# Giving the rotated keys' and queries' tile 128 more bytes per partition, and with it other start addresses to what lies behind it

## The chip, the cores and the metric

The kernel runs on one NeuronCore of a Trainium2 chip. The metric is the device time of one execution in microseconds (us). TensorE (PE in the profile) multiplies matrices; VectorE (DVE), ScalarE (ACT) and GpSimd (POOL) work on elements; SyncE (SP) issues the transfers between the chip's memory (DRAM) and the on-chip buffer (SBUF, 128 partitions). An address in this document is a byte offset within a partition, and it is the same on all 128.

## The reference

The program is a two-layer decoder trunk for 256 tokens of width 1024, all in float32. Each layer is a half-step SwiGLU feed-forward (FFN), a token mixer, a second FFN and a gated input embedding, each followed by a scaled residual and a layer norm:

```python
for i in range(DEPTH):                       # DEPTH = 2
    if i == N_A:
        k_nope, k_rope, v_shared = shared_kv(x, ...)
    x = post_norm(x, 0.5 * swiglu(x, ffn1_w_in[i], ffn1_w_out[i]), ...)
    mix = fox_mixer(x, ...) if i < N_A else mla_mixer(x, ..., k_nope, k_rope, v_shared, cos, sin)
    x = post_norm(x, mix, ...)
    x = post_norm(x, 0.5 * swiglu(x, ffn2_w_in[i], ffn2_w_out[i]), ...)
    gate = sigmoid(x @ ple_w_gate[i] + ple_b_gate[i])
    x = post_norm(x, gate * (p[i] @ ple_w_proj[i]), ...)
```

Layer 0 mixes with forgetting attention (FoX: 16 heads of 64, a decay mask), layer 1 with multi-head latent attention (MLA: 16 heads, keys and values from a shared latent, 128 unrotated and 64 rotated dimensions). The FFN's inner width is 2816.

## The kernel before

**Numbers in two parts.** Every matrix is held as a high part, rounded to TensorE's float32r, and a low part, the rest. A product is three matmuls (`mm3`): high by high, high by low, low by high. Each weight unit arrives in one of three landing buffers (`raw`, 8,192 bytes per partition), ACT writes its high part (line 252) and DVE its low part (line 253) into a buffer of 8,448 bytes, and TensorE reads it from there, as the operand that it loads first (the stationary one) or as the one that streams past (the moving one). In the profile's names, `h<-xT,hl` has the moving operand first and the stationary one behind it. Nearly all matmuls are recorded at line 616, in the helper `mm`.

**The buffers.** Ten buffers (`hl0` to `hl9`) hold split weights only. Four more, named in `HOMES = ("fs", "qk", "ota", "otb")`, and `gb` change their use from stage to stage: now a split weight, now something else. In the FFNs (`ffn`, line 721, with `sums` at line 859) the inner width is cut into 11 chunks. For most chunks eight block sums of the activations (a scheme that needs seven products in place of eight) are put as high and low part in one of the four homes, and `sums` multiplies a chunk's sums, stationary, by the weights' sums, moving: seven products of three matmuls of 512 columns for each chunk, and the chunks take the homes in turn. The cold first FFN has five such chunks, of which one lies in `ota`; each of the three other FFNs has eight, in two groups of four, `fs`, `qk`, `ota`, `otb`. In both mixers `ota` and `otb` hold the attention's output (`OT`), stationary in the output product `O`: 96 matmuls of 512 columns in FoX, and 168 in MLA (its last two heads' outputs lie in `fs`).

**How addresses come about.** A pool gives each name (tag) one place, as large as the largest tile ever asked for under that name, rounded up to 32 bytes, and lays the names out in the order in which they are first asked for. So a tile's size sets where all later names begin. The largest tile under `qk` is the one in `gen` of the MLA stage: the rotated (and unrotated) keys and queries, `[128, 2, 1072]` of 4 bytes, 8,576 bytes, of which columns 0 to 1023 of each half are used. The other large buffers take 8,448 bytes, which is 33 times 256. Small unused tiles (`gap0` to `gap3`) and a shift by 48 words in `Stream.place` (for weights that are the moving operand beside `xT` in the FoX values and the first embedding gate) set other starts.

Start addresses before, modulo 256: `xT` 160; `fs`, `hl0` to `hl9`, `P`, `g4`, `gb`, `ts`, `qk` 224; `ota` (178,272) and `otb` (186,720) 96; `PT` (the transposed attention weights) 160; `p1` (a third block of them) 128; the three `raw` buffers 128.

The order of the work is that of the program text and of the tables `FOX` and `ORDER`; a planner in `Stream` decides, from costs in columns, after which matmul a weight unit is split.

Of the kernel before, what the change touches and what calls it, by code (L numbers as in the profile page):

```python
# [11 lines left out]
F32R = mybir.dt.float32r  # L12
# [498 lines left out]
class Trunk:  # L511
# [990 lines left out]
    def mla(self, li):  # L1502
# [173 lines left out]

        def gen(h):
            if h == 0:
                o = self.own([128, 2, 1072], F32R, "qk")
                home["qk"] = o[:, :, 0:1024].rearrange("p w (t i s c) -> p w t i s c", t=2, i=2, s=2)  # L1680
            ps = self.bank("h")
            hp, s = h // 2, h % 2
            w = self.use(("kvk", hp))
            for k in range(2):
                self.mm3(
                    ps[:, 256:512], lambda i: w[:, i, 256 * k + 128 * s : 256 * k + 128 * s + 128],
                    lambda i: self.ckv[:, :, i, k, :], k == 0, k == 1,
                )
            w = self.use(("qn", hp))
            for k in range(3):  # L1690
                self.mm3(
                    ps[:, 0:256], lambda i: w[:, i, 256 * k + 128 * s : 256 * k + 128 * s + 128],
                    lambda i: cqt[:, :, i, k, :], k == 0, k == 2,
                )
            o = home["qk"]
            left["gen", h] = o[:, :, :, 0, s], o[:, :, :, 1, s], ps.rearrange("p (w t c) -> p w t c", w=2, t=2)
# [108 lines left out]
        def hold(x):  # L1805
            S.hold = bool(x)

        steps = dict(
            dq=dq, rms=rms, dqs=dq_scale, cqT=cq_transpose, V=V, vlo=vlo, qr=q_rope, rope=rope, rc=rope_copy, rot=rotate, zT=zT_first,
            zs=z_split, zU=zT_last, gen=gen, QK=QK, mi=minima, ex=exps, rec=recip, div=divide, T=T, AV=AV,  # L1810
            ga=high("gen"), gd=low("gen"), ta=high("T"), tr=raw_copy, td=low("T"), oa=high("AV"), od=low("AV"), O=O, y=room, hold=hold,
            f=S.fill, a=S.ahead, l=S.later, XT=lambda t, n: self.XT(t, (n,)),
# [122 lines left out]
```

## Time and profile before

| | us |
|---|---|
| median of 3 runs | 1050.32 (1049.77 to 1051.04) |
| the profiled execution | 1049.6 |
| its span, first to last instruction | 1047.8 |
| TensorE busy with matmuls | 1035.6 |
| VectorE busy | 891.8 |
| ScalarE busy | 592.9 |

The granted TensorE clock is full (0.998 in the mean). A row of the profile's timeline gives the start of a group of instructions, its length, engine, line, operation, operands, shapes and count. Matmuls are pipelined: a matmul's own length runs beyond the start of the next one, so what a group costs is read from its start to the start of the group behind it.

### The profile page before, as it was taken

The numbers are of one execution on the slowest core, as the hardware profiler recorded it, in microseconds if no ns is written. First come the engines' busy times: TensorE is split into PE (matmuls) and PEld (weight loads), VectorE is DVE, ScalarE is ACT, GpSimd is POOL, SyncE is SP. The second block draws the span as 40 slices with busy tenths as digits, with TensorE's granted clock in tenths as the row PEclk, the third lists the DMA queues.
The fourth block names the chain that finished last, engine by engine and source line by source line (L and its number), as shares of the span: only waits on it lengthen the run. The fifth ranks groups of instructions, "written<-read, shape, count | busy, mean of one in ns | idle before, by whom it ended". The sixth has DMA issues, their size and how long they took to land.

```text
span 1047.8 us, 17555 instructions
## 1 busy us (share of the span) xinstructions
PE 1035.6 (99%) x7085; PEld 948.6 (91%) x7085; DVE 891.8 (85%) x1312; ACT 592.9 (57%) x901; POOL 58.0 (6%) x88
## 2 busy tenths in 40 slices
PE   9999999999999999999999999999999999999996
PEld 8999898899889999998899898988999889898986
DVE  5788977868898979978979899888887989889877
ACT  6555563666755555663565646646776564646541
POOL 0000000122300000000220000000000000000000
PEclk9999999999999999999999999999999999999999
DMA  7855586455636363673674545743445564555732
GB/s 281 305 191 188 185 298 243 162 168 169 216 128 246 121 252 125 241 282 132 236 260 151 195 169 190 270 142 112 145 156 179 183 214 162 200 190 176 271 125 81
DMA packets 37476, 202.74 MB, mean 193 GB/s; under 512 B 3970, under 2 KB 9874, under 8 KB 16532
## 3 DMA queue, kind: packets, MB, share of 16 engines
q1 hardware_dynamic: 37396, 201.63, 54.3%
q8 instruction: 55, 0.90, 0.3%
q14 instruction: 25, 0.20, 0.1%
HBM read 200.55 MB, written 1.06 MB: 192 GB/s over the span
## 4 chain that ended last, share of the span: by engine, by line
PE 95%; DVE 2%; ACT 1%; issue 1%; DMA 0%; SPq 0%; DVEq 0%; ACTq 0%
PE h L616 53%; PE y L616 29%; PE tr L616 10%; PE tr L620 2%; DVE hl L253 1%; PE h L620 1%; DMA raw<-in_w_dram 0%; PE tr L1375 0%; DVE ts L300 0%; DVE x L705 0%; DVE tr L1720 0%; ACT qk L629 0%; DVE PT L633 0%; DVE ts L306 0%; DVE raw L308 0%
## 5 line engine op out<-in xcount | busy, mean ns | idle before, releaser
L616 PE MATMUL h<-xT,hl 128*128 128x256 f32 x3144 | 366.1, 277 | 1.2 <-ACT hl L327 0.7
L616 PEld LDWEIGHTS h<-xT,hl 128*128 128x128 f32 x3144 | 362.0, 188 | 2.9 <-ACT hl L327 1.2
L253 DVE TENSOR_TENSOR hl<-raw,hl 128x1024 fp32r<-128x1024 f32 (+5 forms) x271 | 314.2, 1190 | 36.1 <-ACT hl L252 35.0
L252 ACT ACTIVATE hl<-raw 128x1024 fp32r<-128x1024 f32 (+5 forms) x271 | 267.8, 1027 | 70.6 <-DVE raw L308 41.3
L616 PE MATMUL y<-hl,g 128*128 128x512 f32 x336 | 78.6, 391 | 0.0
L616 PEld LDWEIGHTS y<-hl,g 128*128 128x128 f32 x336 | 62.5, 188 | 12.6
L616 PE MATMUL h<-hl,xT 128*128 128x512 f32 (+2 forms) x312 | 67.9, 371 | 0.0
L616 PEld LDWEIGHTS h<-hl,xT 128*128 128x128 f32 x312 | 54.9, 188 | 9.8
L616 PE MATMUL y<-hl,otb 128*128 128x512 f32 x219 | 58.0, 399 | 0.0
L264 DVE TENSOR_TENSOR hl<-raw,hl 128x1024 fp32r<-128x1024 f32 (+2 forms) x44 | 52.3, 1192 | 0.8 <-ACT hl L260 0.7
L616 PE MATMUL y<-hl,xT 128*128 128x512 f32 (+3 forms) x282 | 52.7, 334 | 0.0
L260 ACT ACTIVATE hl<-raw 128x1024 fp32r<-128x1024 f32 (+2 forms) x44 | 45.2, 1029 | 9.7 <-DVE raw L308 9.1
L629 ACT ACTIVATE xT<-tr 128x512 fp32r<-128x512 f32 x28 | 16.1, 597 | 58.9 <-PE tr L620 58.9
L616 PEld LDWEIGHTS y<-hl,xT 128*128 128x128 f32 x282 | 44.1, 188 | 4.6 <-ACT xT L629 0.4
L616 PEld LDWEIGHTS y<-hl,otb 128*128 128x128 f32 x219 | 39.8, 188 | 8.4 <-DVE otb L633 0.3
L616 PE MATMUL y<-hl,ota 128*128 128x512 f32 x177 | 46.8, 398 | 0.1
L700 POOL TENSOR_TENSOR rs<-ve,mhalf 128x1 f32<-128x1 f32 x16 | 15.1, 942 | 519.8 <-DVE ve L699 519.8
L616 PE MATMUL tr<-xT,hl 128*128 128x256 f32 x360 | 42.5, 277 | 0.0
L616 PEld LDWEIGHTS tr<-xT,hl 128*128 128x128 f32 x360 | 41.7, 188 | 0.4
L616 PEld LDWEIGHTS y<-hl,ota 128*128 128x128 f32 x177 | 32.7, 189 | 7.7 <-DVE hl L253 0.6
L823 ACT ACTIVATE P<-h 128x512 f32<-128x512 f32 x33 | 19.7, 596 | 33.0 <-PE h L616 32.6
L300 DVE TENSOR_TENSOR ts<-raw 128x1024 f32<-128x1024 f32 x29 | 35.4, 1222 | 0.6
(322 smaller groups left out, 1632.7 us busy)
## 6 DMA issues: line engine op xcount, KB each, us to landing
raw<-in_ffn_in_dram SPq DMA_DIRECT2D x85, 1024.0 KB, 5.0
raw<-in_ffn_out_dram SPq DMA_DIRECT2D x44, 1024.0 KB, 5.0
raw<-in_pg_dram SPq DMA_DIRECT2D x8, 1024.0 KB, 4.9
raw<-in_mo_dram SPq DMA_DIRECT2D x8, 1024.0 KB, 4.8
raw<-in_kq_dram SPq DMA_DIRECT2D x8, 640.0 KB, 4.2
gb<-in_ln_g_dram SPq DMA_DIRECT2D x8, 512.0 KB, 5.9
gb<-in_ln_b_dram SPq DMA_DIRECT2D x8, 512.0 KB, 7.5
raw<-in_fk_dram SPq DMA_DIRECT2D x4, 1024.0 KB, 5.6
```

Source lines behind the costliest of these rows:

```text
L252: nc.scalar.activation(hi, src, AF.Copy)
L253: nc.vector.tensor_tensor(lo, src, hi.bitcast(F32), op=ALU.subtract)
L260: nc.scalar.activation(hi, src, AF.Copy)
L264: nc.vector.tensor_tensor(lo, src, hi.bitcast(F32), op=ALU.subtract)
L300: tt(s[:, 0:1024].rearrange("p (a b) -> p a b", b=512), r[:, 0:512][:, None, :].to_broadcast([128, 2, 512]), r[:, 512:1536].rearrange("p ( ...
L616: self.nc.tensor.matmul(out, lhsT, rhs, start=start, stop=stop)
L620: self.nc.tensor.transpose(out, in_, self.ident)
L629: self.nc.scalar.activation(hi, src, AF.Copy)
L700: nc.gpsimd.tensor_tensor(rs, ve, self.mhalf, op=ALU.pow)
L823: nc.scalar.activation(gt, ps, AF.Silu)
```

## The change

```diff
         def gen(h):
             if h == 0:
-                o = self.own([128, 2, 1072], F32R, "qk")
+                o = self.own([128, 2176], F32R, "qk")[:, 0:2144].rearrange("p (w c) -> p w c", w=2)
                 home["qk"] = o[:, :, 0:1024].rearrange("p w (t i s c) -> p w t i s c", t=2, i=2, s=2)
```

The tile takes 8,704 bytes (34 times 256) in place of 8,576. Its two halves keep their places in it, so all that is read or written in `qk` keeps its address. No instruction is added, taken away or moved on any engine, and no wait is added: the program before and the program after differ in addresses alone. Every name that is laid out behind `qk` begins 128 bytes later:

| | address modulo 256 before | after |
|---|---|---|
| `ota` | 96 | 224 |
| `otb` | 96 | 224 |
| `PT` | 160 | 32 |
| `p1` | 128 | 0 |
| `raw`, all three | 128 | 0 |
| the layer norms' and softmax's small tiles (8 to 128 bytes), `nrm` | various | 128 more |

`xT`, `fs`, `hl0` to `hl9`, `P`, `g4`, `gb`, `ts` and `qk` lie ahead of it and stay.

## The prediction

> **What bounds the kernel now.** I read the page's first and fourth part first.
>
> ```profile
> PE 1035.6 (99%) x7085; PEld 948.6 (91%) x7085; DVE 891.8 (85%) x1312; ACT 592.9 (57%) x901; POOL 58.0 (6%) x88
> PE 95%; DVE 2%; ACT 1%; issue 1%; DMA 0%; SPq 0%; DVEq 0%; ACTq 0%
> ```
>
> TensorE is busy for 1035.6 of the span's 1047.8 us, and 95% of the chain that ends last is its own. So the kernel takes as long as its matmuls take, and what changes a matmul's pace changes the time. The change alters no instruction, only addresses. The question is therefore whether the pace of the matmuls that read `ota` and `otb` depends on where these begin. The timeline of one FFN group shows it, since there four chunks do the same 21 matmuls from four homes:
>
> ```profile
> 409.01 1.54 PE L616 MATMUL y<-hl,fs 128*128 128x512 f32 x6
> ...
> 413.79 1.52 PE L616 MATMUL y<-hl,qk 128*128 128x512 f32 x6
> ...
> 418.55 1.56 PE L616 MATMUL y<-hl,ota 128*128 128x512 f32 x6
> ...
> 423.43 1.56 PE L616 MATMUL y<-gb,otb 128*128 128x512 f32 x6
> ...
> 428.31 0.87 PE L616 MATMUL h<-xT,hl 128*128 128x256 f32 x6
> ```
>
> From start to start the chunk in `fs` takes 4.78 us, in `qk` 4.78, in `ota` 4.88, in `otb` 4.88. `fs` and `qk` begin at 224 modulo 256, as the moving operand's buffers do; `ota` and `otb` begin at 96, 128 bytes off. So 21 matmuls cost 0.10 us more, 5 ns each. Other rows say that it is no matter of these tiles' use as sums. Where `ota` is itself a weight buffer, moving past `g4` at 224:
>
> ```profile
> 154.73 20.56 PE L616 MATMUL y<-hl,g 128*128 128x512 f32 x90
> 175.13 1.55 PE L616 MATMUL y<-ota,g 128*128 128x512 f32 x6
> 176.53 6.98 PE L616 MATMUL y<-hl,g 128*128 128x512 f32 x30
> ```
>
> Ninety matmuls from `hl` take 20.40 us, 226.7 ns each; six from `ota` 1.40 us, 233. And in the first embedding gate, where `place` shifts the weights by 192 bytes so that `qk` is read from 160 and `otb` from 32, beside `xT` at 160:
>
> ```profile
> 487.54 1.55 PE L616 MATMUL y<-otb,xT 128*128 128x512 f32 x6
> 488.94 1.54 PE L616 MATMUL y<-qk,xT 128*128 128x512 f32 x6
> 490.31 1.52 PE L616 MATMUL y<-fs,xT 128*128 128x512 f32 x6
> ```
>
> 1.40 us from `otb`, 1.37 from `qk`. The fast pace is seen at 224 beside 224 and at 160 beside 160, so the two operands' places against each other decide, not an address by itself. Matmuls of 256 columns do not feel it:
>
> ```profile
> L616 PE MATMUL h<-xT,hl 128*128 128x256 f32 x3144 | 366.1, 277 | 1.2 <-ACT hl L327 0.7 <-DVE hl L329 0.4
> L616 PE MATMUL h<-xT,otb 128*128 128x256 f32 x192 | 23.1, 276 | 0.0
> ```
>
> 277 and 276 ns. So the change touches the matmuls of 512 columns that have `ota` or `otb` as an operand, and what it is worth is a count times a few nanoseconds. The Trainium skill, TensorE: Matmul & The Clock Gate, Part 2 (what each phase is for), speaks against that: it gives the array two independent read ports, so that loading the next weights takes nothing from the running matmul. By it the chunks would be equal and the change worth nothing. The chunks' rows differ, and the measurement decides; no row here shows which port or bank is behind it.
>
> **The sums of the FFNs.** Three FFNs have four chunks each in `ota` and `otb`: 12 chunks by 0.10 to 0.12 us. (The chain's own starts for the same four chunks lie 4.78, 4.76 and 4.89 us apart:
>
> ```profile
> 409.17 1.38 PE y L616 x6
> 413.95 1.36 PE y L616 x6
> 418.71 1.39 PE y L616 x6
> 423.60 1.39 PE y L616 x6
> ```
>
> so `qk` against `ota` is 0.13, `fs` against `ota` 0.11.) I take 0.12: 1.44 us. Between these chunks nothing waits, so the gain stays. The cold FFN's one chunk in `ota` is another case:
>
> ```profile
> 112.93 1.15 DVE hl L253
> 114.12 1.42 PE y L616 x5
> ```
>
> ```profile
> 113.59 1.96 PE L616 MATMUL y<-hl,ota 128*128 128x512 f32 x6
> 115.38 0.87 PE L616 MATMUL h<-hl,ota 128*128 128x512 f32 x3
> ```
>
> Its first six matmuls take 1.79 us, 0.39 more than 1.40, because a split on DVE ends late and the chain runs through it. A faster matmul waits longer there: 0.
>
> **The output products.** FoX has 96 such matmuls. In the stretch at its end nothing is between them:
>
> ```profile
> 289.70 2.96 PE L616 MATMUL y<-hl,ota 128*128 128x512 f32 x12
> 292.50 2.96 PE L616 MATMUL y<-hl,otb 128*128 128x512 f32 x12
> 295.30 1.56 PE L616 MATMUL y<-hl,ota 128*128 128x512 f32 x6
> 296.70 1.56 PE L616 MATMUL y<-hl,otb 128*128 128x512 f32 x6
> 298.10 0.60 PE L620 MATMUL tr<-ident,x 128*128 128x128 f32 x4
> ```
>
> 8.40 us for 36 matmuls, 233.3 each. At 226.7 they would save 6.6 ns each, 0.24 us; for all 96 that is 0.63 at most. MLA has 168, and there the trace holds the counter-example, since the last two heads' outputs lie in `fs`, at 224 already:
>
> ```profile
> 819.59 4.40 PE L616 MATMUL y<-hl,fs 128*128 128x512 f32 x18
> 823.82 5.75 PE L616 MATMUL y<-hl,ota 128*128 128x512 f32 x24
> 829.40 0.60 PE L620 MATMUL tr<-ident,x 128*128 128x128 f32 x4
> ```
>
> 18 matmuls from `fs` take 4.23 us, 235 each; 24 from `ota` behind them 5.58, 232.5. The first of the 18 follows matmuls of another kind and carries that, so the 235 is too high for a steady pace, but it shows that a short batch after other work gains little from its address. MLA's products mostly come in batches of 6. Ends: 0, and 168 by 6.6 or 1.1 us. I take 0.15 for MLA, near the row of its own stage, and 0.35 for FoX, between its 0.24 and its 0.63.
>
> **The homes as weight buffers.** As moving operand with 512 columns they stand in 78 matmuls (12 beside `g`, the others beside `xT` or `fs`). The rows above give 0.04 us for six beside `g` (1.40 against 1.36) and 0.03 for six beside `xT` where `place` shifts the weights too. Where it does not, the operands go from 64 bytes apart on one side to 64 on the other, and `qk` stands there today. 13 sixes by 0 to 0.04: 0 to 0.5, and I take 0.2, since only half of them come to the same place as their partner.
>
> **What else moves.** The landing buffers go from 128 to 0, and every split reads them. The trace has that relation already: a split into `otb` reads 128 and writes 96, 32 bytes below, and after the change a split into any `hl` reads 0 and writes 224, 32 bytes below as well.
>
> ```profile
> L253 DVE TENSOR_TENSOR hl<-raw,hl 128x1024 fp32r<-128x1024 f32 x246 | 293.2, 1221 | 33.4 <-ACT hl L252 32.6
> L253 DVE TENSOR_TENSOR otb<-raw,otb 128x1024 fp32r<-128x1024 f32 x13 | 15.8, 1219 | 3.1 <-ACT otb L252 3.1
> ```
>
> 1221 and 1219 ns on DVE: no difference, so I take 0 for the splits. `PT` and `p1`, moving in the attention's second product, have no row at their new places; by the 6.6 ns above on FoX's 24 matmuls of 512 columns the bound is 0.16 us either way, and I take 0. The transfers land at 0 in place of 128:
>
> ```profile
> raw<-in_ffn_in_dram SPq DMA_DIRECT2D x85, 1024.0 KB, 5.0
> ACT hl L327 <- DMA raw<-in_w_dram: 4.0, 5, 2.0
> ```
>
> They are waited for in the first ten microseconds, 4.0 us in five waits; later the buffers are loaded ahead. If landing became a tenth quicker, that would be worth up to 0.4 us, if it does not, nothing; no row shows a transfer that lands at 0, and I take 0.05. The Trainium skill, DMA: Bandwidth & Descriptors, section on how a descriptor splits into AXI transactions, says that a descriptor that does not begin at a multiple of 256 bytes fetches the bytes below it too. An estimate from that page for 8 KB begun at 128 is 260 beats against 256, 1.5%; no run here shows yet whether the receiving side counts.
>
> **The sum.** 1.44 + 0.35 + 0.15 + 0.20 + 0.05 = 2.2 us less. Against the profiled execution's 1049.6 us that is 1047.4; that execution lies 0.7 below the median of the runs shown, 1050.32, so I forecast 1048.1. The bound for a difference that a measurement can tell is 0.2%, 2.1 us: the forecast stands almost on it.
>
> **The rivals.**
>
> *All of it, and the landing too.* The output products keep the FFN's pace: 1.44 + 0.63 + 1.1 + 0.5 + 0.4 = 4.1 us at most, 1046.2; I price it at 3.4, or 1046.9. Against it stands the row of 18 from `fs`.
>
> *The gain is lost, or is not one of addresses.* Either `ota` and `otb` are slow for another reason (they lie highest of the homes, for one) and stay as they are, or faster matmuls only wait for DVE, as they do in the cold FFN: DVE is nearly full in the sums' stretches.
>
> ```profile
> 425.00:450.00 25.00, 25.00 (x205) 24.16 (x205) 24.63 (x28) 16.12 (x19) 0.00 (x0) 1.00 0.79 271
> ```
>
> 24.63 of 25 us. For it also: the page on TensorE. Against it: TensorE has no gap there, and the fast pace at 160 beside 160. 0 to 1.6 us less, 1048.7 to 1050.3; I take 1049.5.
>
> *Slower, by the splits.* Every weight split reads a landing buffer at a new place. In this stretch DVE has 0.37 us to spare, and at 1221 ns at most 20 splits lie in it, so the rival decides from about 18 ns per split on. At 40 ns a stretch would need 0.80 us, 0.43 more than there is; if ten stretches of the run are as full (my assumption) and no split is done ahead, 4.3 us against the gain's 2.2 give 1052.4. The rows of `otb` (1219 against 1221) speak against it.
>
> **How the numbers follow.** My forecast's case (1.6 to 3.0 us less) gets 0.58, the full gain 0.13, the lost gain 0.24, the slower case 0.05. In the forecast's case about seven in ten lie beyond 2.1 us: 0.40, with the full gain 0.53 for faster. Within the bound: 0.18 + 0.24 = 0.42. Slower: 0.05. The range goes from 1046.5, short of the full gain's end, to 1050.1, where most of the lost-gain case is in.
>
> **What would show it.** In the timeline after, the four chunks of a group should take 4.76 to 4.78 us each; six from `ota` beside `g` 1.36; the 36 at FoX's end 8.2; the 18 from `fs` as before and the 24 behind them near 5.5. Splits should stay at 1221 ns on DVE, and the first waits for `raw` at about 4 us. I am wrong in the mechanism if chunks in `ota` still take 4.88; wrong in the size if MLA's batches gain 6 ns per matmul, or if waits of TensorE for DVE grow by what the chunks lose.

## The result, and the profile after

| | before | after |
|---|---|---|
| median of the runs, us | 1050.47 (6 runs, 1049.12 to 1051.04) | 1057.39 (6 runs, 1055.34 to 1058.75) |
| the profiled execution, us | 1049.6 | 1058.75 |
| its span, us | 1047.8 | 1057.0 |

The ratio is 1.0067, with a 95% interval from 1.0054 to 1.008: the change made the kernel slower by about 7 us. The forecast was 1048.1, in a range from 1046.5 to 1050.1, so it was wrong, and in its sign too. No rival had the mechanism that did it.

First the two rows of the page after that answer to those of before, busy time and shares of the chain:

```profile
PE 1038.2 (98%) x7085; PEld 952.0 (90%) x7085; DVE 892.7 (84%) x1312; ACT 594.6 (56%) x901; POOL 58.9 (6%) x88
PE 91%; DVE 5%; ACT 2%; issue 1%; DMA 0%; DVEq 0%; SPq 0%; ACTq 0%
```

The span grew by 9.2 us, but TensorE's busy time only by 2.6. The rest is idle time, and the chain now runs through DVE for 5% where it was 2%. So the question is for what TensorE waits. TensorE's part of the view of waits after (total, times, longest):

```profile
PE tr L616 <- DVE qk L633: 5.2, 4, 1.8
PE tr L616 <- ACT qk L629: 2.3, 3, 1.2
PE y L592 <- POOL mhalf L577: 1.2, 1, 1.2
```

The third row is there before as well. The first two are new: 7.5 us in seven waits of matmuls that read `qk`, for the high and low parts that ACT (line 629) and DVE (line 633) write into `qk`. That tile is the one that the change rewrote, and its addresses did not move.

Next, where in the program it is lost. Two rows of the timeline of TensorE, the first at the start of the MLA stage, the second at its end; first before, then after:

```profile
692.13 0.60 PE L620 MATMUL tr<-ident,x 128*128 128x128 f32 x4
```

```profile
692.15 0.60 PE L620 MATMUL tr<-ident,x 128*128 128x128 f32 x4
...
829.84 4.36 PE L616 MATMUL y<-hl,fs 128*128 128x512 f32 x18
834.04 5.61 PE L616 MATMUL y<-hl,ota 128*128 128x512 f32 x24
839.48 0.60 PE L620 MATMUL tr<-ident,x 128*128 128x128 f32 x4
```

At the start of the MLA stage the two executions stand level, 0.02 us apart: 1.43 us that were lost by 102 us had been won back by then. The 18 products from `fs` at the stage's end start at 829.84, in place of 819.59: 10.25 us later. So the whole of the net loss lies in that stage, and behind it the distance shrinks again, to 9.2 at the end.

One of the waits, in the timeline of all engines. Before, TensorE goes from the transposes of `P` straight into the score product, which reads `qk`; the writes into `qk` that stand beside it go on at the same time:

```profile
750.78 0.49 PE L620 MATMUL tr<-ident,P 128*128 128x128 f32 x3
...
750.98 0.60 ACT L629 ACTIVATE qk<-h 128x512 fp32r<-128x512 f32 x1 [0.23 <-PE h L616]
...
751.03 0.43 PE L616 MATMUL tr<-qk 128*128 128x256 f32 x2
...
752.23 0.68 DVE L633 TENSOR_TENSOR qk<-h,qk 128x512 fp32r<-128x512 f32 x1
```

After, the same place:

```profile
751.30 0.49 PE L620 MATMUL tr<-ident,P 128*128 128x128 f32 x3
...
751.50 0.60 ACT L629 ACTIVATE qk<-h 128x512 fp32r<-128x512 f32 x1 [0.19 <-PE h L616]
...
752.75 0.68 DVE L633 TENSOR_TENSOR qk<-h,qk 128x512 fp32r<-128x512 f32 x1
753.57 0.42 PE L616 MATMUL tr<-qk 128*128 128x256 f32 x2 [1.78 <-DVE qk L633]
```

Before, the score product starts at 751.03, more than a microsecond ahead of DVE's write of the low part: it doesn't need it. After, it starts behind that write. The write belongs to another head: the order of the stage has the projection of head 6 and its two writes (`gen 6`, `ga 6`, `gd 6`) around the score product of head 5 (`QK 5`). From the transposes' start to the product's start it is 2.27 us in place of 0.25.

The program says so too. The instructions on TensorE and their order are the same before and after, but what they wait for is not (- before, + after; the number behind an engine is its semaphore's):

```
-L616 MATMUL tr_7712<-qk 128x256 [waits PE_49]
+L616 MATMUL tr_7712<-qk 128x256 [waits DVE_49]
-L616 MATMUL tr_7953<-qk 128x256 [waits DVE_49]
+L616 MATMUL tr_7953<-qk 128x256 [waits DVE_49,Activation_49]
```

In this way 25 instructions differ on TensorE, 2 on ACT and 3 on DVE (two of these 3 are writes at line 633 that wait for TensorE where they waited for ACT), all of them in the MLA stage. Seven of the 25 are the matmuls that are seen to wait above; `tr_7953` is the one at 753.57. The statement in the section on the change that no wait is added, and that the two programs differ in addresses alone, is therefore wrong. It rested on the list of instructions, which is the same, and on the addresses, and left the waits out.

What was forecast of the addresses did come. The four chunks of the FFN group after:

```profile
409.65 1.54 PE L616 MATMUL y<-hl,fs 128*128 128x512 f32 x6
...
414.43 1.52 PE L616 MATMUL y<-hl,qk 128*128 128x512 f32 x6
...
419.19 1.52 PE L616 MATMUL y<-hl,ota 128*128 128x512 f32 x6
...
423.95 1.52 PE L616 MATMUL y<-gb,otb 128*128 128x512 f32 x6
...
428.71 0.87 PE L616 MATMUL h<-xT,hl 128*128 128x256 f32 x6
```

From start to start 4.78, 4.76, 4.76, 4.76 us: `ota` and `otb` no longer take 4.88. The 36 products at FoX's end take 8.17 us in place of 8.40, 227 ns each, from the first row to the transposes behind them:

```profile
290.83 2.89 PE L616 MATMUL y<-hl,ota 128*128 128x512 f32 x12
...
299.00 0.60 PE L620 MATMUL tr<-ident,x 128*128 128x128 f32 x4
```

And six products from `ota` beside `g` take 1.36, as said (1.40 before):

```profile
176.36 1.52 PE L616 MATMUL y<-ota,g 128*128 128x512 f32 x6
177.72 2.66 PE L616 MATMUL y<-hl,g 128*128 128x512 f32 x11
```

### The profile page after: what moved, and what is told of

Same layout as the page of the kernel before. It is cut to its first block, busy times and chain, and to the rows that moved or that the text cites. A ratio compares the mean times of both kernels' runs of the same rounds, so it can differ in the third digit from the quotient of the medians.

```text
span 1057.0 us, 17555 instructions
## 1 busy us (share of the span) xinstructions
PE 1038.2 (98%) x7085; PEld 952.0 (90%) x7085; DVE 892.7 (84%) x1312; ACT 594.6 (56%) x901; POOL 58.9 (6%) x88
## 4 chain that ended last, share of the span: by engine, by line
PE 91%; DVE 5%; ACT 2%; issue 1%; DMA 0%; DVEq 0%; SPq 0%; ACTq 0%
PE h L616 51%; PE y L616 28%; PE tr L616 10%; PE tr L620 2%; DVE hl L253 1%; PE h L620 1%; ACT qk L629 1%; DVE ts L300 0%; DVE tr L1720 0%; DVE qk L633 0%; DVE PT L633 0%; ACT hl L252 0%; DVE ts L306 0%; DVE raw L308 0%; DVE g L253 0%
```

## The experiments

**The theory (W).** The change has two parts. The addresses gain about what was forecast. The new way of writing the tile, a flat row of 2,176 cut to 2,144 and then seen as two halves of 1,072, makes the framework follow the regions of `qk` more coarsely. The columns of even and odd heads lie in turn in it, in blocks of 128, so a read of one head's block and a write of the neighbour's are taken to overlap, and a wait is put between them. **The rivals:** the new addresses themselves cost time (`PT`, `p1`, the small tiles, or the landing buffers), and the waits are only where it shows; or any flat or larger tile costs it.

The first four kernels take the two parts apart. Each comes with its edit against the kernel before; the kernel before ran on the same chip beside them, with a median of 1050.64. Of the nine programs of this section, the first has exactly the waits of the change; the other eight have those of the kernel before in every instruction.

**Waits without addresses.** A row of 2,208 keeps the form of the change, and moves all names behind it by 256 bytes, so that every address stays as it was, modulo 256.

```diff
-                o = self.own([128, 2, 1072], F32R, "qk")
+                o = self.own([128, 2208], F32R, "qk")[:, 0:2144].rearrange("p (w c) -> p w c", w=2)
```

> The changed program's waits at the old addresses: the tile is asked for as 2,208 columns, cut to 2,144 and seen as two halves, so everything behind qk lies 256 bytes later, the same modulo 256 as before the change. Theory W (the way in which the tile is written makes the program order the score product of one head behind the writes of the neighbouring head, and that costs the time): no address gain is left, so it is slower than the changed kernel by the about 2 us that the addresses give, 1059 to 1060 us, with TensorE waiting for DVE and ACT writes of qk for 6 to 8 us in the latent-attention stage. Theory A (an address that moved makes that stage slow): 1050.5 us, as before the change.

Measured: 1059.39 us, ratio 1.0084 (1.0069 to 1.01). The same seven waits stand in its view of waits, with the same sums:

```profile
PE tr L616 <- DVE qk L633: 5.2, 4, 1.8
PE tr L616 <- ACT qk L629: 2.3, 3, 1.2
```

Followed instruction by instruction, TensorE is 0.47 us behind the kernel before where the MLA mixer's part begins, 9.53 at its end, and 9.53 at the program's end. So the form alone costs 9.1 us, and nothing outside that stage. The view's 7.5 us is less than that because a matmul's modelled length runs past the start of the next: at the place shown above it has 1.78, where 2.02 were lost from start to start. Read from start to start, the seven waits of this kernel cost 0.76, 2.03, 2.09, 0.61, 1.33, 1.38 and 0.83 us, 9.0 together.

**Addresses without waits.** The tile stays as it was, and an unused tile of 128 bytes is laid out behind it.

```diff
+GAPS = {'qk': 32}
...
-        return self.sb.tile(shape, dt, tag=tag, name=tag, bufs=bufs)
+        t = self.sb.tile(shape, dt, tag=tag, name=tag, bufs=bufs)
+        n = GAPS.pop(tag, 0) if not self.rec else 0
+        if n:
+            self.sb.tile([128, n], F32, tag="behind_" + tag, name="behind_" + tag, bufs=1)
+        return t
```

> The changed kernel's addresses with the old waits: the tile stays [128, 2, 1072], and an unused tile of 128 bytes is laid out behind qk. Theory W: the forecast's gain shows alone, 1048.1 us (1047 to 1049), the chunks in ota and otb at 4.77 us. Theory A: as slow as the changed kernel, about 1057 us.

Measured: 1046.44 us, ratio 0.9965 (0.9952 to 0.9977). All of the change's addresses without its waits make the kernel faster by about 4 us. The rival that the addresses cost time falls.

The two parts multiply to 1.0084 × 0.9965 = 1.0049, where the change measured 1.0067 (1.0054 to 1.008). The difference lies within the intervals; a part of it may be the drop of the clock in the change's own executions, which is described further below.

**Addresses, with the landing buffers back at their old places.** `GAPS = {'qk': 32, 'otb': 32}`, the rest as above: `ota`, `otb`, `PT` and the softmax's small tiles as in the change, `nrm`, `p1` and `raw` where they were, modulo 256.

> As the run with the addresses alone, with a second unused tile of 128 bytes behind otb, so that nrm, p1 and the landing buffers begin as before the change, modulo 256 (160, 128, 128); ota, otb, PT and the softmax's small tiles stay moved. Theory W: 1048.1 us again, if landing at 0 or at 128 does not matter; if landing at 0 is what cost the changed kernel's profile 1.2 us in its first 110 us, about 1 us less than the run with the addresses alone. Theory A with the landing buffers as the address that hurts: 1048 us, where the run with the addresses alone has 1057.

Measured: 1047.06 us, ratio 0.9967 (0.9955 to 0.998): the same as with everything moved.

**The landing buffers alone.** `GAPS = {'otb': 32}`.

> Only nrm, p1 and the landing buffers moved by 128 bytes (an unused tile of 128 bytes behind otb); ota, otb, PT and the small tiles where they were, old waits. Theory W: 1050.5 us, within 0.1%, or up to 1 us more if landing at 0 costs the first stage something. Theory A with the landing buffers: 1057 us or more.

Measured: 1050.45 us, ratio 1.0 (0.9991 to 1.0009). Eleven runs show no difference in time, and the row of the transfers is within 0.1 us of the 5.0 before (a kernel with the landing buffers back at 128, the one just above, has 4.9 as well):

```profile
raw<-in_ffn_in_dram SPq DMA_DIRECT2D x85, 1024.0 KB, 4.9
```

The prediction's estimate of 1.5% for a start at 128 was worked out from the Trainium skill, DMA: Bandwidth & Descriptors, section on the split into AXI transactions. No run here can tell whether it holds for the side that receives: 1.5% of 5.0 us is 0.08 us, less than the row's last digit.

The next two kernels mend the change in two ways, and so tell what in its form makes the waits. From here on the kernel before had a median of 1049.26.

**The same room in three dimensions.** The tile takes the change's 8,704 bytes, without a cut (the second half begins 64 bytes later in it).

```diff
-                o = self.own([128, 2, 1072], F32R, "qk")
+                o = self.own([128, 2, 1088], F32R, "qk")
```

> The change written without the cut: the tile is asked for as [128, 2, 1088], 8,704 bytes as in the change, so that all behind it begins where the change puts it, and the waits are the old ones (the second half begins 64 bytes later in the tile, at 224 like the first). Theory W: as the run with the addresses alone, 1046 to 1048 us, 3 to 4 us under before. Theory A in any form: 1057 us.

Measured: 1046.35 us, ratio 0.9972 (0.9963 to 0.9981). Its 18 products at the end of MLA start at 819.07, 0.52 ahead of before's 819.59:

```profile
819.07 4.36 PE L616 MATMUL y<-hl,fs 128*128 128x512 f32 x18
```

So it isn't the tile's size either.

**The change's cut, with the heads apart.** The flat row and the cut at 2,144 stay; even heads lie in the first half and odd ones in the second, so that neighbours no longer lie in turn.

```diff
-                o = self.own([128, 2, 1072], F32R, "qk")
-                home["qk"] = o[:, :, 0:1024].rearrange("p w (t i s c) -> p w t i s c", t=2, i=2, s=2)
+                o = self.own([128, 2176], F32R, "qk")[:, 0:2144].rearrange("p (s c) -> p s c", s=2)
+                home["qk"] = o[:, :, 0:1024].rearrange("p s (w t i c) -> p w t i s c", w=2, t=2, i=2)
```

> The changed kernel's tile and cut word for word ([128, 2176], cut to 2,144, two halves of 1,072), but a half holds all of the even or all of the odd heads' queries and keys, where before each half interleaves even and odd heads in blocks of 128 columns. Theory W, with the overlap of the neighbouring heads' regions as the reason for the waits: no TensorE wait on qk for more than 1 us in total, and 1046 to 1048 us. If the cut itself costs, whatever lies in it: 1056 to 1058 us.

Measured: 1046.89 us, ratio 0.9977 (0.9968 to 0.9986). TensorE's longest waits in it are again those of before, and none is for `qk`:

```profile
PE y L592 <- POOL mhalf L577: 1.2, 1, 1.2
PE h L616 <- ACT hl L327: 0.6, 1, 0.6
PE h L616 <- ACT p L629: 0.5, 1, 0.5
```

The cut costs nothing by itself. It costs where regions lie in turn that belong to different heads. Theory W stands. (Two more forms, a flat row of 2,144 without a cut and a row of 2,176 in two halves of 1,088, have before's waits in the program; they were not run. How the framework comes to its coarser view of the cut row is open.)

The last three kernels are on the addresses: whether what counts is the distance of the two operands, and whether more can be had from it.

**Sixty-four bytes apart.** `GAPS = {'qk': 16, 'otb': 48}`: `ota` and `otb` at 160, beside moving operands at 224.

> ota and otb at 160 modulo 256, 64 bytes from the moving operand's 224, and PT at 224; the landing buffers, nrm and p1 as before; old waits. If the pace follows the distance of the two operands modulo 256, a chunk in ota or otb takes between 4.77 and 4.88, near 4.82 us (xT at 160 beside 224 gave 229 ns where the same place gave 226.7), and the time is 1.3 to 1.8 us under before, about 1049. If only the one place 128 bytes off is slow, 4.77 and 1047 us; if anything but the same place is slow, 4.88 and 1050.5 us.

Measured: 1052.33 us, ratio 1.0028 (1.0017 to 1.0039). The four chunks came out half way, as expected:

```profile
411.54 1.54 PE L621 MATMUL y<-hl,fs 128*128 128x512 f32 x6
...
416.32 1.52 PE L621 MATMUL y<-hl,qk 128*128 128x512 f32 x6
...
421.08 1.54 PE L621 MATMUL y<-hl,ota 128*128 128x512 f32 x6
...
425.88 1.53 PE L621 MATMUL y<-gb,otb 128*128 128x512 f32 x6
...
430.69 0.87 PE L621 MATMUL h<-xT,hl 128*128 128x256 f32 x6
```

4.78, 4.76, 4.80, 4.81. The time as a whole did not: it is slower than before, and the expectation of the total missed. At 160 these homes stand at the place of `xT`, and the matmuls of 256 columns that stream `xT` past them feel that. Here, and then with the homes at 224 (the kernel with the addresses alone), 24 such matmuls:

```profile
561.36 3.04 PE L621 MATMUL h<-xT,otb 128*128 128x256 f32 x24
564.24 1.93 PE L621 MATMUL h<-xT,hl 128*128 128x256 f32 x15
```

```profile
557.16 2.88 PE L621 MATMUL h<-xT,otb 128*128 128x256 f32 x24
559.88 1.30 PE L621 MATMUL h<-xT,hl 128*128 128x256 f32 x10
```

2.88 us against 2.72, or 120 ns against 113. These 288 matmuls would account for 2 us. The rest lies in stretches that run at 118 ns: of 168 blocks of 24 matmuls that stream `xT`, 65 have a median over 116 ns (288 matmuls, or 12 such blocks, are those beside the homes themselves), and 11 in the kernel with the addresses alone. Of the 65, 30 lie behind 330 us, nearly all beside or just behind such a home, and no other trace has more than 2 there. Another 19 lie before 62 us, ahead of the first of these homes (147.5 us), so the homes aren't their cause.

**More weights at the place of `xT`.** On top of the mended change, the shift in `place` holds for all the weights that are read beside `xT`.

```diff
-    return key[0] == "fv" or key[:2] == ("pg", 0)
+    return key[0] in ("fv", "pg", "win")
```

> The three-dimensional wider tile, and on top the shift by 48 words for all weights of 512 columns that move beside xT (the first chunk of the FFNs and both embedding gates in place of the FoX values and the first gate), so that they begin at 160 like xT. About 340 matmuls that ran at 229 to 230 ns should come to 227: 0.8 to 1.0 us less than the run without it, 1045.5 to 1046.5 us. A rival: these stretches wait for the splits and nothing is gained.

Measured: 1046.59 us, ratio 0.9976 (0.9966 to 0.9986), no better than the mended change alone. The 512-column matmuls beside `xT` went from 229 to 227 ns, but the last embedding gate works in pieces of 256, and so does the cold first FFN's first chunk. In the last gate, this kernel and then the mended change alone:

```profile
1025.31 0.52 PE L616 MATMUL y<-otb,xT 128*128 128x256 f32 x3
1025.67 0.52 PE L616 MATMUL y<-qk,xT 128*128 128x256 f32 x3
```

```profile
1027.35 0.50 PE L616 MATMUL y<-otb,xT 128*128 128x256 f32 x3
1027.69 0.50 PE L616 MATMUL y<-qk,xT 128*128 128x256 f32 x3
```

Three take 0.36 us at the same place and 0.34 at 64 bytes off. So the 336 matmuls of 512 columns gained about 0.7 us, and 96 in the last gate lost about 0.6 of it (120 ns in place of 113); the 96 of the cold chunk run at 120 as well.

**The same, without the cold chunk.**

```diff
-    return key[0] == "fv" or key[:2] == ("pg", 0)
+    return key[0] in ("fv", "pg") or key[0] == "win" and key[1:3] != (0, "ffn1")
```

> As the run with more places met, but the cold first FFN's first chunk is left at 224: there the weights are the stationary operand of 256-column matmuls with xT moving, and at xT's own place those ran at 120 ns in place of 113. 96 matmuls by 7 ns come back, and the first stage no longer starts in the slow pace of 118 ns: 0.6 to 1.2 us under the run with more places met, 1045.4 to 1046 us, 4 us under before and the fastest of all. A rival: the first stage's pace is left to chance and the two cannot be told apart, 1046.5 us.

Measured, beside a kernel before of 1049.43: 1047.24 us, ratio 0.9979 (0.997 to 0.9987). It can't be told apart from the mended change: another miss. The best version found is thus the change's room in three dimensions, or the unused tile behind `qk`: both about 3 to 4 us faster than the kernel before, and some 10 faster than the change.

## Why the prediction was wrong

The step that failed is the sentence "The change alters no instruction, only addresses", and with it the rivals, which were all about addresses. Every number after it was worked out for a program that the change did not make: waits between instructions had no term in the sum, and there they cost 9.1 us with the old addresses. In the profiled execution of the change the MLA mixer's part costs 10.3 (TensorE stands 0.05 ahead of the kernel before at its start and 10.22 behind at its end); the last part of that is a drop of the granted clock just behind the wait shown above. In windows of 5 us (TensorE, its weight loads, DVE, ACT, GpSimd, then the clock), the change, then the kernel with the waits alone:

```profile
750.00:755.00 5.00, 3.22 (x24) 3.01 (x23) 2.85 (x7) 3.69 (x9) 0.00 (x0) 0.90 0.02 3
755.00:760.00 5.00, 5.00 (x24) 4.22 (x23) 3.89 (x11) 3.34 (x9) 0.00 (x0) 0.76 0.26 80
```

```profile
750.00:755.00 5.00, 3.22 (x28) 3.01 (x27) 3.39 (x7) 4.05 (x12) 0.00 (x0) 1.00 0.09 39
755.00:760.00 5.00, 5.00 (x33) 4.49 (x33) 3.83 (x11) 3.47 (x10) 0.00 (x0) 1.00 0.24 63
```

0.90 and 0.76 against 1.00 with the same wait in both: the drop belongs to that execution and isn't shown to follow from the wait. The profiled execution is also the longest of the six; the median is 1.4 lower. Of the other five only the mean clock is known. It is 0.998 in the fastest (1055.34 us) and 0.996 or 0.997 in the rest, so drops like this one may lie in them too.

The terms of the sum, where the addresses were tried alone:

| term | forecast | measured |
|---|---|---|
| sums of the FFNs | 1.44 | 1.44 in the chunks (12 by 0.12); 0.24 of it lost again in one group, to two blocks at 118 ns |
| FoX's output products | 0.35 | 0.4 |
| MLA's output products | 0.15 | 0.4 to 0.5 |
| homes as weight buffers | 0.20 | 0.2 in the matmuls that stream them; 0.3 more in the other matmuls of the last gate |
| landing | 0.05 | 0 (0.9991 to 1.0009) |
| all | 2.2 | 4.2 with the unused tile (2.4 to 5.0), 2.9 in three dimensions (2.0 to 3.9) |

So this half of the argument held, and was if anything priced too low. The batches in MLA did gain: the 24 from `ota` take 5.44 us (834.04 to 839.48) in place of 5.58, though the row of 18 from `fs`, 4.23 before and 4.20 after, had seemed to say that they would not. All 168 gained 0.4 to 0.5 us in the traces, or about 2.7 ns each, less than half of the 6.6 that a steady pace would give. The matmuls of 256 columns in the last gate were not in the sum at all. The step "matmuls of 256 columns do not feel it" read more from its two rows than they hold: both compare places 64 bytes from `xT` (96 and 224 beside 160). At the place of `xT` itself they do feel it, as the kernel with the homes at 160 shows.

What is above the terms' total, near 2.8, in the medians is within the intervals and within what single traces differ by: stretches of the `xT` matmuls that run at 118 ns in place of 113 come and go from trace to trace. The change's own profile stands 1.43 behind before's at 102 us, with 12 blocks of 24 at 118 ns from 71 us on; the kernel with the addresses alone, whose program is the same up to there, has none of them.

The rival "slower, by the splits" had the right sign and the wrong mechanism: splits on DVE take 1222 ns after, 1221 before.

```profile
L253 DVE TENSOR_TENSOR hl<-raw,hl 128x1024 fp32r<-128x1024 f32 x246 | 293.3, 1222 | 34.3 <-ACT hl L252 33.4
```

The rival "not one of addresses" falls by the kernel that moves addresses and nothing else. The same chunks go from 4.88 to 4.76 us there as in the change, and a place half way gives 4.80 and 4.81. The Trainium skill, TensorE: Matmul & The Clock Gate, Part 2 (what each phase is for), with its two independent read ports would have had them equal; the measurement decides against it for these operands. What in the memory or in TensorE makes the dependence is still open.

What would have shown it ahead of time was there to be had: the waits of the changed program, set beside those of the program before. The prediction named "waits of TensorE for DVE" as a sign of its being wrong, but as the price of faster matmuls, not as something that the new line of code brings.

## What to carry to other kernels

Where a framework puts in the waits, a change of how a tile is written (cut, flattened, seen in other dimensions) is a change of the program's waits until the two lists of waits have been compared; here one cut cost 9 us and the addresses behind it gave 3 to 4. Room for an address is better made by an unused tile or by a wider dimension, which leave the views as they were. And where addresses are chosen, each shape of matmul is to be measured: the place that is best for 512 columns is the worst of those tried for 256 columns.

## What the hardware showed that was not expected

- Matmuls of 512 columns depend on the start of the stationary and the moving operand modulo 256. From start to start, in medians over the traces, they take 227 ns where both begin at the same place (both at 224, or both at 160), 229 where the moving one begins at 224 and the stationary one at 160, and 231 to 232 where they are 128 bytes apart. The distance isn't all: with the moving one at 96 and the stationary one at 160, also 64 bytes, 24 matmuls took 233 in the kernel with the homes at 160.
- What runs before counts too. Six from `otb`, moving at 160 beside `xT` at 160, took 227 ns each where the matmuls before them moved weights at 160 as well (the kernel with more weights at the place of `xT`), and 232 where those lay at 224 (the kernel with the homes at 160).
- Matmuls of 256 columns go the other way: those that stream `xT` in two pieces of 128 take 113 ns with the stationary operand at 96 or 224 beside `xT` at 160, and 120 at 160. In one piece, with `xT` stationary, those of the last gate take 120 ns with the weights at 160 too, and 113 with all weights at 224.
- The same matmuls have a second pace, 118 ns, that lasts for tens of matmuls: 9 of 168 blocks in the profile before, 23 after, 31 in the one of the three dimensions, 65 with the homes at 160 (of which those beside the homes are 12). One place where it starts shows in the last gate. In the kernel before, the weights there lie at 224, but those in `otb` at 96:

```profile
1027.85 0.84 PE L616 MATMUL y<-hl,xT 128*128 128x256 f32 x6
1028.53 0.52 PE L616 MATMUL y<-otb,xT 128*128 128x256 f32 x3
1028.88 0.52 PE L616 MATMUL y<-qk,xT 128*128 128x256 f32 x3
1029.24 0.52 PE L616 MATMUL y<-fs,xT 128*128 128x256 f32 x3
```

  The first six take 113 ns each. From the three of `otb` on it is 117 to 119, also for `qk`, `fs` and `hl` at 224, to the end of the gate. With `otb` at 224 the whole gate runs at 113 (the rows of the mended change above). What starts the pace elsewhere, and what ends it, is open.
- Whether a transfer lands at 0 or at 128 modulo 256 made no difference to its row (4.9 and 5.0 us) or to the time.
